# Binding the fetched-expert work behind its dense block on VectorE, and giving stored activations their own buffers

## The chip, the cores and the metric

One NeuronCore of a Trainium2 chip runs the whole program. The metric is the device time of one execution in microseconds. Before the change the median of three runs was 4709.95 us (4702.84 to 4711.42).

## What is computed

Two transformer-like blocks over 512 tokens of width 1024 in float32. The part that matters here is the expert layer ("PEER") of the first block. For each token and each of 8 heads, two top-16 searches over 128 keys give 16 of 16384 experts with softmax gates; the layer is a sum over these 128 experts per token:

```python
u_sel = u_tab[idx]
v_sel = v_tab[idx]
act = jax.nn.gelu(jnp.einsum('td,thkd->thk', hb, u_sel), approximate=False) * gate
return jnp.einsum('thk,thkd->td', act, v_sel)
```

The kernel computes it in two ways. For the last 384 tokens it is dense: all 16384 experts are evaluated in 128 blocks of 128, `gelu(u_tab @ x)` is multiplied by a matrix W that holds the gates (zero where an expert is not chosen), and the product goes through `v_tab`. For the first 128 tokens only the chosen rows of both tables are fetched: 128 rows of each table per token.

## The kernel before

Every float32 matrix product is made of three matmuls of rounded operands: `split` (L288) writes a high part with a cast on ScalarE (L294) and a low part with a subtraction on VectorE (L295), and `mm3` (L298) issues high x high, low x high and high x low (L300 to L302; names in the profile end in H and L). A weight tile is loaded in pairs (`wraw`, 1024 KB, two buffers) and split into `wd` or `we`.

`phase_b` calls three generators that are woven together by hand.

- `peer_select` (L1131) routes the tokens, and beside that computes the first NU = 56 of the 128 blocks of activations (`peer_act`, L1260: 24 matmuls of 384 columns, then a Gelu into a tile `pge`, three buffers) and stores them in HBM (`geD`). The matrix W goes to HBM too (`WD`).
- `peer_dense` (L1276) takes all 128 blocks in groups of four. A group is either *stored* (14 groups: its activations are loaded back from `geD` by `spilled`, L1286) or *fresh* (18 groups: `peer_act` computes them now, on PSUM bank `sb`); the two kinds alternate about evenly, and the last two groups are a stored and a fresh one. Each block's activations are multiplied by W in place (L1298, tile `pW`, one load per group), split into `pG` (three buffers), and drive 18 matmuls of 512 columns against the split rows of `v_tab` (`praw`, 1024 KB for two blocks, two buffers; `pV`, two buffers). The sums stay in six PSUM banks until the end.
- `peer_own` (L1085) is the work on fetched experts: 256 steps, each with one row of an expert table per token (128 x 1024 floats, 512 KB, an indirect DMA from GpSimd, L1111) in a ring of AHEAD = 4 buffers `pfr`. A step with a row of `u_tab` is a multiply-and-reduce on VectorE (L1119), a step with a row of `v_tab` a multiply-and-add into `pfo` (L1127); the order is 16 of the first kind, then alternately 16 and 16. After 16 dot products come a Gelu on ScalarE and a multiplication. The buffer freed by step k takes the row of step k + 4.

The steps of `peer_own` are handed out by counts. `peer_select` takes one per stored block from the fourth on, so `taken` is 53. `peer_dense` gets the other 203: a pace of 0.85 for a block that is followed by a stored one and 2.3 for one that is followed by a fresh one, scaled so that all are written by the 122nd block (L1312 to L1329).

What is written is not what is issued: the framework orders each engine's instructions by a priority that follows the program's order, among those that its own timing model holds ready. An instruction written later can so be issued earlier when the model sees its engine idle and its operands there. The order so found is fixed at build time; in the trace each engine's instructions run in one such order, and one that waits holds up those behind it. `issue_after(ins)` adds, for every instruction traced inside the block on the engine of `ins`, the condition that it be issued behind `ins`; it adds no instruction and no semaphore, and says nothing of instructions on other engines.

In the loop of `peer_dense`, the operands of block i + 1 (`nxt = next(G, None)`) are written before the matmuls of block i, and the own steps after them:

```python
(gh, gl), (vh, vl) = nxt, next(Vh)
nxt = next(G, None)
due += pace(i) * left / total
while gone < min(due, left):
    next(own)
    gone += 1
```

Of the kernel before, what the change touches and what calls it, by code (L numbers as in the profile page):

```python
# [9 lines left out]
F32 = mybir.dt.float32  # L10
# [20 lines left out]
TD = T - 128  # L31
# [221 lines left out]
class Kern:  # L253
# [34 lines left out]
    def split(self, pool, x, name, shape=None, bufs=1, l_eng=None):  # L288

        nc = self.nc  # L290
        shape = shape or list(x.shape)
        h = pool.tile(shape, F32R, name=name + 'H', bufs=bufs)
        l = pool.tile(shape, F32R, name=name + 'L', bufs=bufs)
        nc.scalar.copy(h, x)  # L294
        (l_eng or nc.vector).tensor_sub(l, x, h.bitcast(F32))  # L295
        return h, l

    def mm3(self, out, wh, wl, xh, xl, start, stop):  # L298
# [977 lines left out]
    def peer_dense(self, pd, f2, r, st, own):  # L1276


        nc, ap = self.nc, self.ap
        J = 4  # L1280

        ng, ns = 128 // J, NU // J
        order = sorted(range(ng), key=lambda i: (i + 0.5) / ns if i < ns else (i - ns + 0.5) / (ng - ns))
        fresh = self.peer_act(pd, f2, NU, 128 - NU, tag=('sb', 2))

        def spilled(grp):  # L1286
            for b in range(J * grp, J * grp + J):
                ge = pd.tile([128, TD], F32, name='pge', bufs=3)
                nc.sync.dma_start(ge, self.geD[b])
                yield b, ge  # L1290

        def acts():
            for grp in order:
                W = pd.tile([128, 12, J, 32], F32, name='pW', bufs=2)
                nc.sync.dma_start(W, self.WD[:, :, J * grp:J * grp + J, :])
                for b, ge in spilled(grp) if J * grp < NU else islice(fresh, J):
                    gv = ge.rearrange('p (a b) -> p a b', a=12)
                    nc.vector.tensor_mul(gv, gv, W[:, :, b % J])  # L1298
                    yield self.split(pd, ge, 'pG', bufs=3)

        def values():
            for grp in order:
                for i in range(0, J, 2):
                    raw = pd.tile([128, 2, 1024], F32, name='praw', bufs=2)
                    nc.sync.dma_start(raw, ap['pv'][128 * (J * grp + i):128 * (J * grp + i + 2)].rearrange('(t p) f -> p t f', t=2))
                    for q in range(2):
                        yield self.split(pd, raw[:, q], 'pV', bufs=2)

        acc = [[self.mmps() for _ in range(2)] for _ in range(2)] + [[self.mmps('sa', 2) for _ in range(2)]]
        G, Vh = acts(), values()  # L1310

        blocks = [grp * J >= NU for grp in order for _ in range(J)] + [False]  # L1312
        pace = lambda i: 2.3 if blocks[i + 1] else 0.85
        left = 256 - self.taken
        total = sum(pace(i) for i in range(122))
        due, gone = 0.0, 0
        nxt = next(G)
        for i in range(128):
            (gh, gl), (vh, vl) = nxt, next(Vh)
            nxt = next(G, None)  # L1320
            due += pace(i) * left / total

            for t, h in ([(t, h) for t in range(3) for h in range(2)] if i < 127 else [(t, h) for h in range(2) for t in range(3)]):
                s, c = slice(t * 128, t * 128 + 128), slice(h * 512, h * 512 + 512)
                self.mm3(acc[t][h], gh[:, s], gl[:, s], vh[:, c], vl[:, c], i == 0, i == 127)
            while gone < min(due, left):
                next(own)
                gone += 1
        for _ in own:  # L1329
            pass  # L1330

        o = [self.own] + [pd.tile([128, 1024], F32, name=f'po{t}') for t in range(3)]
        for h in range(2):
            c = slice(h * 512, h * 512 + 512)
            for t in range(3):
                (nc.scalar.copy, nc.vector.tensor_copy)[t % 2](o[t + 1][:, c], acc[t][h])
            for d in range(4 * h, 4 * h + 4):
                ps = self.mmps('sb', 2)
                for t in range(4):
                    nc.tensor.transpose(ps[:, t * 128:t * 128 + 128], o[t][:, d * 128:d * 128 + 128], self.ident)  # L1340
                nc.vector.scalar_tensor_tensor(r[:, d], ps, self.M[:, 40 + d, 0:1], r[:, d], op0=OP.mult, op1=OP.add)
                st.tile(d)
# [973 lines left out]
```

## Time and profile before

| | |
|---|---|
| median of three runs | 4709.95 us |
| the profiled execution, its own time | 4711.78 us |
| its span | 4709.2 us |
| busy: TensorE / VectorE / ScalarE / GpSimd | 93% / 58% / 35% / 22% |
| mean granted clock of TensorE | 0.959 of full speed |
| HBM traffic over the span | 137 GB/s |
| `peer_dense`: first and last multiplication by W (L1298) start at | 1482.5 and 2400.9 us |

The busy shares are means over stages with different limits. The stage of the change is about a fifth of the span, and it is read by itself, in two halves that look different: up to about 1960 us and from there on. A row of a wait says who waited, for whom, how long in total and how often. TensorE's matmuls are pipelined, so the sum of their durations is more than the time they take; what one costs in a full pipeline is read from the distance between starts.

### The profile page before, as it was taken

Reading aid. Unit: us, or ns where it says so; the run is one execution under the profiler, and the core shown is the slowest. Engines: PE = TensorE matmul, PEld = TensorE weight load, DVE = VectorE, ACT = ScalarE, POOL = GpSimd, SP = SyncE. Lnnn points to the kernel's source line nnn. Section 1 sums busy time; section 2 is a strip of 40 time slices with the busy share of each in tenths; the row PEclk is TensorE's granted clock in tenths of the full one; section 3 lists DMA queues with packets and bytes.
Section 4 is the critical chain, followed back from the end, with each engine's and each line's share of the span. In section 5 each row is a group of like instructions: output and inputs, shape, how many; then the busy total and the mean of one; then the engine's idle time right before and its main releaser. Section 6 shows DMA issues by size and latency. Waiting matters only on the chain. (4 is left out here: it accounts for less than half of the span.)

```text
span 4709.2 us, 58774 instructions
## 1 busy us (share of the span) xinstructions
PE 4389.7 (93%) x22821; PEld 3698.9 (79%) x22821; DVE 2741.0 (58%) x5167; ACT 1666.0 (35%) x2540; POOL 1048.5 (22%) x880
## 2 busy tenths in 40 slices
PE   7898998988887888999999999999999999999998
PEld 5776777878786776888878887788888888778887
DVE  5676577599987787644443357643343376636333
ACT  3533222326652222333332237332232242323222
POOL 3222343248784454200010021000110010001001
PEclk8899999999998999999999999999999999999999
DMA  6233423336679999745422222122322220011222
GB/s 220 81 97 110 146 106 128 117 113 227 231 272 350 328 327 334 253 170 177 172 70 99 94 90 90 59 90 98 100 81 98 92 76 15 16 45 63 99 95 75
DMA packets 226771, 647.50 MB, mean 137 GB/s; under 512 B 15587, under 2 KB 81395, under 8 KB 220092
## 3 DMA queue, kind: packets, MB, share of 16 engines
q1 hardware_dynamic: 188124, 502.18, 30.9%
q0 software_dynamic: 38368, 141.58, 8.3%
q8 instruction: 179, 2.93, 0.3%
q14 instruction: 100, 0.82, 0.1%
HBM read 590.66 MB, written 53.04 MB: 137 GB/s over the span
## 5 line engine op out<-in xcount | busy, mean ns | idle before, releaser
L302 PE MATMUL mm<-xH,wdL 128*128 128x512 f32 (+4 forms) x2276 | 850.3, 374 | 27.4 <-DVE wdL L295 27.2
L300 PE MATMUL mm<-xH,wdH 128*128 128x512 f32 (+4 forms) x2276 | 854.4, 378 | 15.0 <-DVE cacc L543 9.4
L301 PE MATMUL mm<-xL,wdH 128*128 128x512 f32 (+4 forms) x2276 | 850.4, 374 | 2.7 <-POOL xL L2292 1.5
L294 ACT CAST wdH<-wraw 128x1024 fp32r<-128x1024 f32 (+2 forms) x382 | 395.0, 1035 | 1156.1 <-PE mm L301 750.7
L295 DVE TENSOR_TENSOR wdL<-wraw,wdH 128x1024 fp32r<-128x1024 f32 (+2 forms) x346 | 421.7, 1219 | 460.5 <-ACT wdH L294 447.9
L302 PEld LDWEIGHTS mm<-xH,wdL 128*128 128x128 f32 (+2 forms) x2276 | 435.4, 191 | 99.1 <-DVE wdL L295 32.8
L300 PEld LDWEIGHTS mm<-xH,wdH 128*128 128x128 f32 (+2 forms) x2276 | 435.3, 192 | 86.6 <-issue 13.4
L301 PEld LDWEIGHTS mm<-xL,wdH 128*128 128x128 f32 (+2 forms) x2276 | 436.2, 192 | 70.0 <-POOL xL L2292 3.2
L294 ACT CAST weH<-wraw 128x1024 fp32r<-128x1024 f32 (+2 forms) x162 | 168.1, 1038 | 489.5 <-PE mm L301 302.7
L295 DVE TENSOR_TENSOR weL<-wraw,weH 128x1024 fp32r<-128x1024 f32 (+1 forms) x155 | 189.7, 1224 | 241.2 <-ACT weH L294 215.5
L300 PE MATMUL mm<-xH,weH 128*128 128x512 f32 (+2 forms) x856 | 319.5, 373 | 5.5 <-ACT weH L294 3.9
L302 PE MATMUL mm<-xH,weL 128*128 128x512 f32 (+2 forms) x856 | 316.6, 370 | 5.2 <-DVE weL L295 5.1
L301 PE MATMUL mm<-xL,weH 128*128 128x512 f32 (+2 forms) x856 | 317.5, 371 | 1.2 <-POOL xL L2292 1.1
L300 PE MATMUL mm<-pVH,pGH 128*128 128x512 f32 x512 | 210.8, 413 | 57.1 <-ACT pGH L294 48.4
L2210 POOL TENSOR_TENSOR nsa<-r 128x512 f32<-128x512 f32 x4 | 7.7, 1935 | 1042.9 <-DVE r L1373 1042.9
L2292 POOL TENSOR_TENSOR xL<-r,xH 128x256 fp32r<-128x256 f32 (+1 forms) x84 | 68.9, 832 | 760.1 <-DVE r L2279 499.7
L1366 DVE TENSOR_TENSOR fg<-fg,mm 128x512 f32<-128x512 f32 x88 | 60.5, 687 | 283.8 <-PE mm L302 283.1
L301 PE MATMUL mm<-pVL,pGH 128*128 128x512 f32 x512 | 210.7, 412 | 10.6 <-DVE pVL L295 10.6
L302 PE MATMUL mm<-pVH,pGL 128*128 128x512 f32 x512 | 212.2, 414 | 7.7 <-DVE pGL L295 7.5
L295 DVE TENSOR_TENSOR pVL<-praw,pVH 128x1024 fp32r<-128x1024 f32 x128 | 156.4, 1222 | 98.2 <-ACT pVH L294 98.2
L1111 POOL DMA_INDIRECT pfr<-in_pun_dram,pfI x128 | 167.6, 1310 | 154.9 <-DVE pfD L1119 90.4
L1111 POOL DMA_INDIRECT pfr<-in_pv_dram,pfI x128 | 164.9, 1289 | 158.6 <-DVE pfo L1127 103.2
(1244 smaller groups left out, 10041.7 us busy)
## 6 DMA issues: line engine op xcount, KB each, us to landing
wraw<-in_wi_dram SPq DMA_DIRECT2D x88, 1024.0 KB, 4.9
praw<-in_pv_dram SPq DMA_DIRECT2D x64, 1024.0 KB, 6.3
wraw<-in_pu_dram SPq DMA_DIRECT2D x63, 1024.0 KB, 6.0
wraw<-in_wmod_dram SPq DMA_DIRECT2D x24, 1024.0 KB, 6.7
wraw<-in_win_dram SPq DMA_DIRECT2D x24, 1024.0 KB, 5.7
WD<-W SPq DMA_DIRECT2D x12, 2048.0 KB
pW<-WD SPq DMA_DIRECT2D x32, 768.0 KB, 5.7
wraw<-in_wo_dram SPq DMA_DIRECT2D x16, 1024.0 KB, 5.0
```

What stands on the lines that cost most here:

```text
L294: nc.scalar.copy(h, x)
L295: (l_eng or nc.vector).tensor_sub(l, x, h.bitcast(F32))
L300: mm(out, wh, xh, start=start, stop=False)
L301: mm(out, wh, xl, start=False, stop=False)
L302: mm(out, wl, xh, start=False, stop=stop)
L1111: nc.gpsimd.indirect_dma_start(out=row, out_offset=None, in_=ap[n], in_offset=bass.IndirectOffsetOnAxis(ap=self.ownI[:, k:k + 1], axis=0))
L1366: nc.vector.tensor_mul(g, g, pss[0])
L2210: self.eng.tensor_add(self.sa, r[:, 0], r[:, 1])
L2292: eng.tensor_sub(l[:, k, s], F[k], h[:, k, s].bitcast(F32))
```

## The change

`split` keeps the VectorE subtraction that it issued last. In `peer_dense` the loop notes it after the operands of block i + 1 are written (so it is the subtraction that makes `pGL` of block i + 1), and the own steps written beside block i are bound behind it in VectorE's order. The stored activations get a tile name of their own, `pgs`, with four buffers; before, they shared the three buffers `pge` with the fresh ones, which now keep these for themselves.

```diff
-        (l_eng or nc.vector).tensor_sub(l, x, h.bitcast(F32))
+        self.last_split = (l_eng or nc.vector).tensor_sub(l, x, h.bitcast(F32)).ins
...
-                ge = pd.tile([128, TD], F32, name='pge', bufs=3)
+                ge = pd.tile([128, TD], F32, name='pgs', bufs=4)
                 nc.sync.dma_start(ge, self.geD[b])
...
             nxt = next(G, None)
+            mark = self.last_split
             due += pace(i) * left / total
...
             while gone < min(due, left):
-                next(own)
+                with self.tc.issue_after(mark):
+                    next(own)
                 gone += 1
```

## Rows read from the trace of the kernel before

**Rows 1.** the page's 40 slices: busy tenths of TensorE and of the DMA engines

```profile
PE   7898998988887888999999999999999999999998
...
DMA  6233423336679999745422222122322220011222
```

**Rows 2.** stretches: us, busy of PE, PEld, DVE, ACT, POOL; clock, DMA share, GB/s

```profile
1400.00:1480.00 80.00, 62.67 (x313) 59.69 (x311) 56.45 (x67) 17.57 (x27) 45.73 (x35) 0.91 0.95 345
1480.00:1960.00 480.00, 405.62 (x1778) 338.09 (x1779) 371.61 (x465) 132.97 (x186) 218.15 (x169) 0.92 0.90 329
1640.00:1680.00 40.00, 38.24 (x174) 32.72 (x174) 28.81 (x40) 10.40 (x14) 17.70 (x14) 0.95 0.86 312
1880.00:1920.00 40.00, 36.41 (x170) 31.65 (x170) 31.57 (x32) 11.34 (x15) 17.68 (x15) 0.96 0.85 314
1960.00:2400.00 440.00, 440.00 (x2151) 390.83 (x2150) 198.05 (x241) 159.43 (x214) 0.00 (x0) 1.00 0.49 164
```

**Rows 3.** the costliest group of TensorE's instructions, 1480 to 1960 us

```profile
L302 PE MATMUL mm<-pVH,pGL 128*128 128x512 f32 x236 | 104.0, 441 | 7.7 <-DVE pGL L295 7.5
```

**Rows 4.** timeline of TensorE around 2005 us: start, duration

```profile
2001.75 0.39 PE L300 MATMUL mm<-pVH,pGH 128*128 128x512 f32 x1
...
2005.87 0.33 PE L300 MATMUL sb<-xH,wdH 128*128 128x384 f32 x1
...
2010.06 0.39 PE L300 MATMUL mm<-pVH,pGH 128*128 128x512 f32 x1
```

**Rows 5.** row buffer pfr, 1400-1482, then 1482-2420 us: ns, first and last start

```profile
L1119 DVE CUSTOM_DVE_ANT_0 pfr<-pfr,pfh x19: 1215/1220/1226, 1399.5 to 1479.6; 128x1024 f32<-128x1024 f32 x19
L1127 DVE SCALAR_TENSOR_TENSOR pfo<-pfr,pfD,pfo x16: 1278/1284/1318, 1433.6 to 1467.6; 128x1024 f32<-128x1024 f32 x16
...
L1127 DVE SCALAR_TENSOR_TENSOR pfo<-pfr,pfD,pfo x96: 1271/1280/1325, 1525.3 to 1952.3; 128x1024 f32<-128x1024 f32 x96
L1119 DVE CUSTOM_DVE_ANT_0 pfr<-pfr,pfh x75: 1214/1220/1227, 1485.5 to 1857.3; 128x1024 f32<-128x1024 f32 x75
```

**Rows 6.** who waited for whom, 1480 to 1960 us: total us, times, longest

```profile
ACT pGH L294 <- DVE pge L1298: 258.0, 58, 9.5
...
PE mm L300 <- ACT pGH L294: 48.4, 17, 7.3
...
ACT pfD L1122 <- DVE pfD L1119: 11.5, 5, 6.8
```

**Rows 7.** DMA, 1480-1960: queues (packets, MB, share); issues (count, KB, us to landing)

```profile
q0 software_dynamic: 24507, 89.19, 50.5%
q1 hardware_dynamic: 41932, 68.35, 39.7%
...
praw<-in_pv_dram SPq DMA_DIRECT2D x30, 1024.0 KB, 9.6
wraw<-in_pu_dram SPq DMA_DIRECT2D x16, 1024.0 KB, 9.1
pW<-WD SPq DMA_DIRECT2D x15, 768.0 KB, 9.9
pge<-geD SPq DMA_DIRECT2D x28, 192.0 KB, 7.8
```

**Rows 8.** groups of VectorE's instructions, 1480-1960 us: busy, mean ns, idle

```profile
L1127 DVE SCALAR_TENSOR_TENSOR pfo<-pfr,pfD,pfo 128x1024 f32<-128x1024 f32 x96 | 123.0, 1281 | 38.3 <-DMA pfr<-in_pv_dram,pfI 37.8
L1119 DVE CUSTOM_DVE_ANT_0 pfr<-pfr,pfh 128x1024 f32<-128x1024 f32 x76 | 92.0, 1221 | 30.3 <-DMA pfr<-in_pun_dram,pfI 30.2
L295 DVE TENSOR_TENSOR pVL<-praw,pVH 128x1024 fp32r<-128x1024 f32 x61 | 74.3, 1219 | 6.8 <-ACT pVH L294 6.8
L1298 DVE TENSOR_TENSOR pge<-pge,pW 128x384 f32<-128x384 f32 x60 | 33.1, 553 | 30.4 <-DMA pge<-geD 28.8 <-DMA pW<-WD 1.6
L295 DVE TENSOR_TENSOR pGL<-pge,pGH 128x384 fp32r<-128x384 f32 x60 | 32.8, 551 | 1.2 <-ACT pGH L294 1.2
```

**Rows 9.** waits of SyncE's DMA queue, 1467 to 2420 us

```profile
SPq L1289 <- DVE pGL L295: 47.2, 23, 4.4
```

## The prediction

> **What bounds the kernel now.** I read the page's slices first. In slices 13 to 16 (1413 to 1884 us) TensorE is at seven or eight tenths and the DMA engines at nine; in slices 18 to 20 TensorE is at nine and the DMA engines at four or five [rows 1]. So the stage has a half that is short of transfers and one that is not. The stretches say how much: from 1480 to 1960 us TensorE is busy 405.62 of 480 us at a mean granted clock of 0.92 (between its two levels, 1.2 and 2.4 GHz) with the DMA engines at 0.90; from 1960 to 2400 us it is busy for all 440 us at 1.00, DMA at 0.49 [rows 2]. GpSimd, which does nothing here but fetch expert rows, has 169 instructions in the first half and none in the second.
>
> What the matmuls would take in a full pipeline comes from the timeline in the undisturbed half. 18 matmuls of 512 columns take 2005.87 - 2001.75 = 4.12 us (0.229 each), 24 of 384 columns 4.19 us (0.1746 each) [rows 4]. In the first half each of the three lines has 236 of the first kind on four of the six banks [rows 3], so 354 on all, 3 x 354 = 1062 in all, and 1778 - 1062 = 716 of the second [rows 2]: 243 + 125 = 368 us of work in 480 us. **112 us are lost there**, as idle time and as time at the lower clock that follows it. In the 80 us ahead of it (the last stored blocks of the selection, 313 matmuls of 384 columns) the work is 54.6 us, so 25 us are lost, at a DMA share of 0.95. Together 137 us; the second half loses nothing.
>
> The rows of the fetched experts say why. 171 own steps run after 1482 us, the last at 1952 us [rows 5]; 256 - 171 = 85 had run before, where only 53 are written. So 32 of the 35 steps between 1400 and 1482 us belong to dense blocks not yet begun, and all 256 are done when VectorE has split 61 of the 128 value blocks [rows 8], where the pace as written ends at the 122nd. In that half VectorE idles 37.8 us ahead of L1127 waiting for rows and 28.8 us ahead of L1298 for stored activations [rows 8]; ScalarE's cast behind L1298 waits 258.0 us, and 48.4 us of that reach TensorE [rows 6]. The steps come too early and too dense: they saturate the DMA engines, and VectorE, waiting in order for a late row, holds back the operands of the next block.
>
> **The change, part by part.** *The noted instruction* is bookkeeping at build time: 0 us.
>
> *The binding* adds no instruction and no wait; it forbids VectorE to issue a step written beside block i ahead of `pGL` of block i + 1. Some 203 steps then spread over 122 blocks. By the pace that is 0.85 for a stored block and 2.3 for a fresh one (54 x 0.85 + 68 x 2.3 = 202, so the scale is 1.00), over some 56 x 4.12 + 72 x 8.31 = 829 us of matmuls.
>
> First the 25 us ahead of the stage. Without the 32 rows (32 x 0.524 = 16.8 MB of the 27.6 that 345 GB/s move in 80 us) the DMA share falls from 0.95 to about 0.4, below the 0.49 at which TensorE never waits. I take all 25; the lower end is 10, if what is left waits on VectorE instead.
>
> Then the stage. Per block the transfers are [rows 7]: `praw` 0.524 MB, `pW` 0.197, for a stored block `pge` 0.197, for a fresh one `wraw` 0.524, and 0.524 per row. A stored block: 0.918 + 0.446 = 1.364 MB in 4.12 us, 331 GB/s; a fresh one: 1.245 + 1.21 = 2.455 MB in 8.31 us, 295 GB/s. Full share is 329 / 0.90 = 366 GB/s [rows 2], so the shares would be 0.90 and 0.81. What a row costs TensorE at a share is bounded by three rows. At 0.90 it is 112 / 171 = 0.65 us. In the two calmer stretches, share 0.86 and 0.85, I count 174 and 170 matmuls at the half's mean of 368 / 1778 = 0.207 us, 36.0 and 35.2 of 40 us, so 4.0 and 4.8 us for 14 and 15 rows: about 0.30 us each [rows 2]. At 0.49, without rows, nothing is lost. I price the 46 rows beside stored blocks at 0.65 (30 us), and the 157 beside fresh ones, below the calm stretches in share and at 0.28 rows per us against 0.36, at a quarter of 0.30 (11 us). **41 us stay of 137; the gain is 96.** The ends are 0 (gain 137) and 0.30 for all (61 us, gain 76); the 0.65 for all is a rival.
>
> What hides the rest: VectorE's load beside a stored block is 1.22 + 0.55 + 0.55 + 0.85 x 1.27 = 3.4 of 4.12 us, beside a fresh one 2.3 + 1.2 + 2.3 x 1.27 = 6.5 of 8.31 [rows 8]. It fits, but VectorE at 0.8 is late next, and a row that comes 1 us late beside a fresh block is still covered, two of 2 us are not. GpSimd's 256 fetches stay and are not bound; each waits for the buffer of the step four before, so with steps 3.6 to 4.8 us apart a row has some 14 us to land in. ScalarE's Gelu on 16 dots waits 11.5 us in 5 cases now, casts queued behind it [rows 6]; there are 6 or 7 such Gelus now instead of 5, the same price. The last steps are written two stored and four fresh blocks before the end, 41 us ahead of the transposes that read `pfo`.
>
> *The own buffers* cost 6 KB per partition and no instruction. The 56 loads leave SyncE's queue when the stored block four earlier is split, not when any of the last three blocks is; a group is loaded while the fresh group before it runs. That takes away the 28.8 us ahead of L1298 and most of the 47.2 us for which SyncE's queue stands still with `praw`, `pW` and `wraw` behind it [rows 9]; both are in the 112. Memory of the stage moves a little, so its first loads may wait for another tile of the selection: 0, with plus or minus 8 us as bounds (the longest wait of TensorE there is 7.3 [rows 6]).
>
> Sum: 4711.78 - 96 = 4616 for the profiled execution, which lies 1.8 us above the median: **4614 us.**
>
> A rule speaks for a higher price. The two queues held the engines 50.5% and 39.7% of the first half [rows 7]: the fetched rows, with a buffer always free, took more than half. The Trainium skill (DMA: Bandwidth & Descriptors, Queues, rings and completion order) says that each DMA engine takes turns, packet by packet, between the queues that have work for it. By that rule, with rows always queued, a stored block's 0.918 MB get half of 366 GB/s and take 5.0 us, 0.9 us too long; over 56 blocks 49 us would stay, a gain of 88. The trace agrees so far as both queues share nearly evenly; whether paced rows still keep the queue full no row shows.
>
> **The rivals.** *Stored groups stay short of transfers.* For it: 331 GB/s is what the saturated half moved. Against it: a stored group lasts only 16.5 us, and `praw`, `pW` and now `pgs` are a group ahead. Stored blocks at half of the engines' time (0.9 us each, 49 us) and fresh rows at the calm stretches' 0.30 (47 us) leave 96: gain 41, 4669 us.
>
> *The cost follows the row, not the crowding.* VectorE waits in order, and steps bound directly ahead of the next block's subtractions would now do so in the half where TensorE never waits. Each row then costs what it costs today, wherever it runs. It decides at 137 / 203 = 0.675 us per row: at 0.65 the gain is 5 (4705 us, no change); at the 25.4 / 35 = 0.73 of 1400 to 1482 us, 148 us are paid for 137: **slower, 4721 us.** Against it: the calm stretches pay half for as many rows.
>
> *The binding does not hold the steps back*, because rows already fetched move the crowding elsewhere. Then only the stored loads' part of VectorE's waits goes: 28.8 of 28.8 + 37.8 + 30.2 [rows 8], 30% of 112, 33 us: 4677 us. Against it: only four rows can be in flight.
>
> **How the numbers follow.** Forecast 0.71 (own range 4573 to 4640: gain 137 to 70); stored groups short 0.15; cost per row 0.09, half of it slower; no hold 0.05. Under 0.2% (9 us) a measurement of this kernel cannot tell a gain from none. Faster 0.91, same 0.05, slower 0.04. From 4578 to 4670 us lie nearly all of the forecast and about half of the first rival; above lie the rest.
>
> **What would show it.** Right: own steps on VectorE last to about 40 us before the stage's end; GpSimd busy through the stage; DMA share near 0.82 throughout; the stage's first and last L1298 some 850 us apart, not 918; the 80 us ahead of it shorter by 25; the wait for stored loads gone; landing of `praw` below 9.6 us. Wrong: the last own step still well ahead of the end, TensorE's idle spread over the whole stage behind L1127 and L1119, or a DMA share above 0.9 in stored groups.

## The result, and the profile after

The changed kernel takes 4583.03 us (median of 4 runs, 4576.06 to 4595.06) against 4710.0 us: a ratio of 0.9736 with the 95% interval [0.9709, 0.9763], 127 us faster. The prediction was 4614 us (4578 to 4670), so the result lies near the lower end of its range; on another chip, beside the first experiments, the same kernel gave 4578.69 us, 0.9729 [0.9705, 0.9754].

The page's slices after, to set beside [rows 1]:

```profile
span 4574.3 us, 58699 instructions
...
PE   7898899997889999999999999999999999999998
...
DMA  6233423336568888888423222222232210011222
```

The DMA engines no longer stand at nine tenths for four slices and at four or five soon behind them; they stand at eight for seven slices, and TensorE is at nine in each of these. The same in stretches (length, busy us of PE, PEld, DVE, ACT, POOL, granted clock, DMA share, GB/s), to set beside [rows 2]: the stage up to the last own step, the whole stage, and what follows the last own step.

```profile
1441.00:2223.00 782.00, 774.16 (x3750) 682.35 (x3749) 582.20 (x732) 280.99 (x385) 287.05 (x199) 1.00 0.87 308
1441.00:2265.00 824.00, 816.16 (x3956) 719.90 (x3955) 600.61 (x753) 295.63 (x403) 287.05 (x199) 1.00 0.84 297
2223.00:2265.00 42.00, 42.00 (x208) 37.56 (x207) 18.41 (x22) 14.64 (x20) 0.00 (x0) 1.00 0.29 101
```

TensorE is busy for 816 of 824 us at a granted clock of 1.00, the upper of its two levels, while the DMA engines carry 0.87 for 782 us. That is nearly the 0.90 of the old first half, which lost nearly a quarter of its 480 us (112 us).

The stored groups can be read by themselves, as the stretches of some 20 us in which bank `sb` gets next to no matmul, so that only the products with `v_tab` run (length, busy, clock, share and GB/s as above). Three of the fourteen:

```profile
1611.22:1631.50 20.28, 20.28 (x91) 16.74 (x90) 15.94 (x17) 7.70 (x11) 9.85 (x7) 1.00 0.96 336
...
1881.16:1901.44 20.28, 20.28 (x91) 16.73 (x90) 15.65 (x18) 7.69 (x11) 9.91 (x7) 1.00 1.01 365
...
2115.39:2135.68 20.29, 20.29 (x92) 16.74 (x91) 16.75 (x21) 7.71 (x11) 10.45 (x8) 1.00 0.99 369
```

In all of them but the last, which has next to no rows left, the DMA share is 0.93 to 1.04, and TensorE idles for under 2 us in each, in most not at all.

The own steps of the stage, with first and last start (compare [rows 5]):

```profile
L1127 DVE SCALAR_TENSOR_TENSOR pfo<-pfr,pfD,pfo x112: 1273/1279/1323, 1490.3 to 2223.8; 128x1024 f32<-128x1024 f32 x112
L1119 DVE CUSTOM_DVE_ANT_0 pfr<-pfr,pfh x91: 1211/1219/1227, 1446.4 to 2106.8; 128x1024 f32<-128x1024 f32 x91
```

All 203 lie in the stage now, and the last starts at 2223.8 us, 41 us before the last Gelu of the stage. VectorE hardly waits for their rows any more (1441 to 2223 us, compare [rows 8]):

```profile
L1127 DVE SCALAR_TENSOR_TENSOR pfo<-pfr,pfD,pfo 128x1024 f32<-128x1024 f32 x111 | 142.4, 1283 | 1.0
L1119 DVE CUSTOM_DVE_ANT_0 pfr<-pfr,pfh 128x1024 f32<-128x1024 f32 x91 | 108.2, 1219 | 5.8 <-DMA pfr<-in_pun_dram,pfI 5.8
...
L1298 DVE TENSOR_TENSOR pgs<-pgs,pW 128x384 f32<-128x384 f32 x56 | 29.5, 554 | 61.2 <-DMA pgs<-geD 48.5 <-DMA pW<-WD 12.5
```

38.3 and 30.3 us of idle time ahead of the own steps became 1.0 and 5.8. The wait for stored activations did not go: it grew from 28.8 to 48.5 us. But little of it reaches TensorE. Waits of the stage (total us, times, longest), the two longest and TensorE's own, to set beside [rows 6]:

```profile
POOL pfr L1111 <- DVE pfD L1119: 254.0, 49, 50.3
POOL pfr L1111 <- DVE pfo L1127: 251.7, 76, 14.6
...
PE mm L301 <- DVE pVL L295: 6.0, 6, 2.6
...
PE mm L300 <- ACT pGH L294: 1.8, 1, 1.8
```

TensorE waits 7.8 us in all where it waited 48.4 us for one cast alone; the longest waiter is now GpSimd, 505.7 us, for row buffers that VectorE has not yet used. Such waits alone are no sign that a pace holds: the run with no own step in the selection (below) has 502.0 us of them and loses 63 us. In the queues' shares, beside [rows 7], the fetched rows had 50.5% of the DMA engines against 39.7%, and have the smaller part now.

```profile
q1 hardware_dynamic: 82176, 135.61, 49.1%
q0 software_dynamic: 28656, 104.35, 37.2%
```

Where the time went is read from ScalarE's Gelus: those of the selection write from bank `mm`, those of the stage from `sb`. Before:

```profile
L1273 ACT ACTIVATE pge<-sb x72: 475/485/492, 1464.9 to 2399.6; 128x384 f32<-128x384 f32 x72
L1273 ACT ACTIVATE pge<-mm x56: 478/484/493, 1022.3 to 1463.5; 128x384 f32<-128x384 f32 x56
```

and after:

```profile
L1273 ACT ACTIVATE pge<-sb x72: 477/485/487, 1438.1 to 2264.9; 128x384 f32<-128x384 f32 x72
...
L1273 ACT ACTIVATE pge<-mm x56: 478/484/493, 1010.5 to 1433.9; 128x384 f32<-128x384 f32 x56
```

The selection went from 441.2 to 423.4 us, the stage from 934.7 to 826.8 us. These two make 126 us, the measured gain. The profiled execution also reaches the selection 11.8 us earlier, in a part that the change does not touch; other executions of kernels with the same earlier part reach it between 1010.5 and 1027.4 us, so that is a matter of the execution, and from here on I use the two lengths.

### The profile page after: what moved, and what is told of

Its sections match the earlier page's. It is cut to its first block, busy times and chain, and to the rows that moved or that the text cites. A ratio compares the mean times of both kernels' runs of the same rounds, so it can differ in the third digit from the quotient of the medians.

```text
span 4574.3 us, 58699 instructions
## 1 busy us (share of the span) xinstructions
PE 4337.6 (95%) x22821; PEld 3672.4 (80%) x22821; DVE 2737.0 (60%) x5167; ACT 1668.0 (36%) x2540; POOL 1079.5 (24%) x880
## 5 line engine op out<-in xcount | busy, mean ns | idle before, releaser
L1111 POOL DMA_INDIRECT pfr<-in_pun_dram,pfI x128 | 181.2, 1416 | 296.3 <-DVE pfD L1119 204.9
L1111 POOL DMA_INDIRECT pfr<-in_pv_dram,pfI x128 | 178.7, 1396 | 269.6 <-DVE pfo L1127 193.2
L302 PE MATMUL mm<-pVH,pGL 128*128 128x512 f32 x512 | 201.3, 393 | 0.0
L300 PE MATMUL mm<-pVH,pGH 128*128 128x512 f32 x512 | 196.4, 390 | 1.8 <-ACT pGH L294 1.8
L300 PEld LDWEIGHTS mm<-xH,weH 128*128 128x128 f32 x856 | 162.5, 190 | 31.6 <-ACT weH L294 4.6
```

The costliest lines, as they stand in the source:

```text
L300: mm(out, wh, xh, start=start, stop=False)
L302: mm(out, wl, xh, start=False, stop=stop)
L1111: nc.gpsimd.indirect_dma_start(out=row, out_offset=None, in_=ap[n], in_offset=bass.IndirectOffsetOnAxis(ap=self.ownI[:, k:k + 1], axis=0))
```

## The experiments

Each kernel was timed in three rounds beside the kernel before (4708 to 4710 us in the three sets) and profiled once. A summary, with the two lengths read as above:

| | median us | ratio to before, 95% | selection us | stage us |
|---|---|---|---|---|
| before | 4710.0 | | 441.2 | 934.7 |
| changed kernel, again | 4578.7 | 0.9729 [0.9705, 0.9754] | 420.3 | 826.0 |
| binding alone | 4628.8 | 0.9842 [0.9824, 0.9861] | 422.7 | 868.0 |
| own buffers alone | 4716.4 | 1.0015 [1.0000, 1.0030] | 443.6 | 941.9 |
| bound at the stage's start only | 4684.2 | 0.9956 [0.9941, 0.9971] | 422.4 | 929.1 |
| no own steps in the stage | 4570.4 | 0.9698 [0.9678, 0.9718] | 423.5 | 814.4 |
| bound, twice the pace | 4694.5 | 0.9968 [0.9953, 0.9983] | 423.9 | 937.5 |
| before, without the fetches | 4561.8 | 0.9676 [0.9653, 0.9698] | 407.7 | 817.8 |
| one ring of seven buffers | 4623.2 | 0.9812 [0.9796, 0.9828] | 422.0 | 869.0 |
| 26 steps in the selection | 4561.9 | 0.9680 [0.9660, 0.9699] | 394.6 | 834.4 |
| the same, flatter pace | 4574.5 | 0.9708 [0.9691, 0.9725] | 394.6 | 845.3 |
| 14 steps, flatter pace | 4592.2 | 0.9749 [0.9733, 0.9766] | 393.8 | 864.8 |
| none, flatter pace | 4608.4 | 0.9786 [0.9770, 0.9802] | 389.8 | 877.8 |

**The changed kernel again.**

> The changed kernel once more, on the chip of the next three. About 4583 us, 4576 to 4595 as before. Open beside it: in the profiles the selection begins 11.5 us earlier than before the change, in a part of the program that the change does not touch. If that is chance of one execution, this profile puts the first Gelu of the selection anywhere between 1010 and 1022 us; if the change moves the earlier order, it is near 1010 again.

4578.69 us, and the first Gelu of the selection starts at 1019.3 us: chance.

### Which of the two parts does it

**The binding alone.**

```diff
-                ge = pd.tile([128, TD], F32, name='pgs', bufs=4)
+                ge = pd.tile([128, TD], F32, name='pge', bufs=3)
```

> The binding alone, stored and fresh activations sharing three buffers as before. Theory (the steps came too early and too dense; the order is all): 4585 to 4600, at most 15 us above the changed kernel. Rival (the stored loads have a share of their own, priced at 28.8 of 96.8 us of VectorE's waits, 33 us): about 4615.

4628.8 us: a gain of 81, and 46 to 50 us short of both parts together. That is more than either theory gave the buffers. The waits of the stage in this kernel:

```profile
DVE pge L1298 <- DMA pge<-geD: 46.6, 16, 4.7
...
PE mm L300 <- ACT pGH L294: 20.0, 14, 2.8
PE mm L301 <- DVE pVL L295: 14.1, 11, 1.8
```

The wait for stored activations is no longer than in the changed kernel (46.6 against 48.5 us), and yet TensorE now waits 34.1 us where it waited 7.8. The place in VectorE's order accounts for that in the case that I followed. In this one of the 16 the loads leave SyncE's queue at 1568.20 us

```profile
1568.20 3.63 SPq L1289 DMA_DIRECT2D pge<-geD  x3
```

and the multiplication by W that needs the first of them stands directly in front of the split that the next matmuls need:

```profile
1577.54 0.56 DVE L1298 TENSOR_TENSOR pge<-pge,pW 128x384 f32<-128x384 f32 x1 [3.76 <-DMA pge<-geD]
1578.01 1.22 DVE L295 TENSOR_TENSOR pVL<-praw,pVH 128x1024 fp32r<-128x1024 f32 x1
```

In the changed kernel the stored tiles run far ahead:

```profile
L1298 DVE TENSOR_TENSOR pgs<-pgs,pW x56: 546/553/561, 1457.2 to 2186.3; 128x384 f32<-128x384 f32 x56
L294 ACT CAST pGH<-pgs x56: 506/516/518, 1461.2 to 2226.6; 128x384 fp32r<-128x384 f32 x56
```

The last of them is multiplied at 2186.3 us and cast at 2226.6 us, 40 us later; only the first four stand less than 25 us ahead of their casts. Waits in front of work that is this early cost TensorE next to nothing. The same idle row of VectorE is a cost in one kernel and none in the other, and its length does not tell which.

**The own buffers alone.**

```diff
-                with self.tc.issue_after(mark):
-                    next(own)
+                next(own)
```

> The four own buffers alone, no binding. Theory (order is all): 4700 to 4710, since VectorE still waits for rows that come late. Rival (a third of the loss is the stored loads): about 4677.

4716.4 us, no gain at all. From 1480 to 1960 us VectorE still waits 66.8 us for rows (68.0 before), its wait for stored activations is 31.2 us (28.8 before), and TensorE's for the cast behind L1298 is no shorter than in [rows 6]:

```profile
PE mm L300 <- ACT pGH L294: 55.1, 20, 7.3
```

The buffers are worth 46 to 50 us, but only once the binding has made room.

**More buffers, or a line of their own?**

```diff
-                ge = pd.tile([128, TD], F32, name='pgs', bufs=4)
+                ge = pd.tile([128, TD], F32, name='pge', bufs=7)
...
-            ge = tp.tile([128, TD], F32, name='pge', bufs=3)
+            ge = tp.tile([128, TD], F32, name='pge', bufs=3 if tag[0] == 'mm' else 7)
```

> The changed kernel with one shared ring of seven activation buffers instead of three and four. With one ring of three (the binding alone) the first load of a stored group leaves only when a fresh block has given a buffer back, 5.6 us before it is needed. Theory (the loads leave too late for want of free buffers): seven shared ones do as well as three and four, 4575 to 4595. Rival (what counts is that fresh and stored tiles do not wait in one line): 4610 to 4630 as with three.

4623.2 us: seven buffers in one ring do no better than three. My theory of too few buffers falls. The loads of a stored group now leave together, with no wait for a buffer in SyncE's queue, but still late:

```profile
1581.49 0.37 SPq L1305 DMA_DIRECT2D praw<-in_pv_dram  x1
1581.91 2.63 SPq L1289 DMA_DIRECT2D pge<-geD  x4
```

ScalarE's Gelu of the fresh block ahead of that group starts at 1582.24 us, 0.3 us from there, and VectorE's multiplication waits for the load until 1590.57 us. In one ring the tiles are handed out in the order in which they are written, so a load would not leave ahead of the fresh tile that is written before it. That reading fits the two times, but it is argued, not shown: in SyncE's queue the four loads also stand right behind a load of `praw` that had waited 5.7 us for its own buffer (first line), so the place in that queue would do as well. Shown is that seven buffers in one ring gain nothing over three, and three and four in two rings do; how many the ring of their own needs was not tried.

**Bound at the stage's start only.**

```diff
-            mark = self.last_split
+            mark = self.last_split if i == 0 else mark
```

> All own steps of the dense stage bound behind the first dense block only: none can run in the selection, but within the stage they are free to run early. Theory (crowding inside the stage costs 0.65 us per row, the selection's tail 25 to 29 us): the tail is gained back, but 203 rows instead of 171 crowd the first half, 32 x 0.65 = 21 us more, so 4695 to 4705. Rival (most of the gain is the tail and the start of the stage): about 4620.

4684.2 us, better than I expected. The selection has the changed kernel's length, so all of its 18 to 21 us come from keeping the 32 steps out of it. In the stage the crowding is back:

```profile
1445.00:1988.00 543.00, 468.44 (x2098) 392.94 (x2097) 429.32 (x542) 152.09 (x216) 271.75 (x199) 0.94 0.92 334
```

By the prediction's 0.207 us per matmul that is 434 us of work in 543, so 109 us for 203 rows, 0.54 each instead of the 0.65 that I put in.

### Transfers, VectorE's time, or the place of a step

**The steps without their fetches.** The kernel before, with three rows fetched once and read by every step:

```diff
-            row = rows[i]
+            row = rows[i % AHEAD]
...
-            fetch(i + AHEAD)
             yield
```

(AHEAD is 3 here, and the first kind of step writes its product to a tile of its own.)

> The kernel before, but only the first three rows are ever fetched and each own step reads one of them (so the sum for the first 128 tokens is another); all VectorE work of the steps stays, as early as the order makes it. Theory (transfers): VectorE alone has about 396 us of work in a half of 368, so some 28 us stay lost of 137: about 4600. Rival (VectorE's time for the early steps is the cost, not the transfers): 4690 to 4710.

4561.8 us. The steps are even earlier than before (the last starts at 1796.7 us instead of 1952.3), VectorE is busy for 79.7 of 80 us ahead of the stage, and TensorE hardly waits:

```profile
1400.00:1480.00 80.00, 79.69 (x418) 73.98 (x417) 79.72 (x103) 31.07 (x45) 0.00 (x0) 1.00 0.67 231
1480.00:1900.00 420.00, 418.69 (x2035) 369.55 (x2034) 359.25 (x449) 152.86 (x206) 0.00 (x0) 1.00 0.51 170
```

So neither early issue nor VectorE's time is the cost. Nearly the whole loss of the stage goes with the transfers (817.8 us against 814.4 with no own steps at all, below), and even the 28 us that I left to VectorE were not there. (The selection is without its fetches too, so the two kernels differ there by more than crowding.)

**Bound, but twice as dense.**

```diff
-        total = sum(pace(i) for i in range(122))
+        total = sum(pace(i) for i in range(61))
```

> The changed kernel with twice the pace: all 203 steps are written beside the first 61 blocks, still bound behind them and with the own buffers. Theory (transfers are what is short): 203 x 0.524 + 27 x 0.918 + 34 x 1.245 = 173 MB in 395 us of matmuls, at 366 GB/s 474 us, so 79 us lost: about 4660. Rival (the place of a step behind the block's operands is what saves, crowding is harmless): only VectorE's load counts, 440 us in 395, 45 us lost: about 4625, or 4585 if even that spreads.

4694.5 us. Every step is behind its block's operands and the stored activations have their buffers, and 112 to 116 us of the gain are gone:

```profile
1440.00:1900.00 460.00, 391.09 (x1713) 329.17 (x1712) 358.48 (x466) 128.00 (x178) 234.65 (x175) 0.92 0.92 335
```

The place of a step does not save the gain; what counts is how much the transfers ask for at a time. And the rate at which they saturate is not the 366 GB/s that I had from 329 / 0.90. The saturated stretches moved 329 GB/s before, 334 and 335 GB/s in these two kernels, with the DMA share at 0.90 to 0.92. By this kernel's own 335 GB/s the 173 MB of the expectation take 516 us for 395 us of matmuls: 121 us lost, and its stage lies 123 us above the 814.4 us of the next run.

**No own steps.**

```diff
-        left = 256 - self.taken
+        left = 0
...
-        for _ in own:
-            pass
```

> The changed kernel with the 203 own steps of the dense stage left out (no fetch, no work on VectorE; the first 128 tokens lack them). It is the floor of the stage. In the profile of the changed kernel the stage takes 824 us where its matmuls need 814.5, so if that count is right the floor is 4568 to 4575, about 10 us below the changed kernel, and a paced row costs 0.05 us. If the rows cost the 0.20 us each of the prediction, the floor is near 4540.

4570.4 us, and a stage of 814.4 us, 12 us shorter than the changed kernel's, in which a count of its matmuls at the prediction's two rates had shown 9.6 us lost of 824. By the medians 203 paced rows cost 8 to 13 us, 0.04 to 0.06 us each.

### How far the room goes

I took VectorE to bound part of the selection; then moving own steps from there into the stage should gain until the stage's transfers saturate.

**26 steps in the selection, 230 in the stage.**

```diff
-                if n > 9:
+                if n > 90:
```

> The changed kernel with 26 own steps instead of 53 taken in the selection, so 230 in the dense stage. From 1040 to 1390 us VectorE is busy for 38 to 39.9 of 40 us in most stretches, so 27 steps of 1.25 us less should shorten that by up to 33 us, and the stage pays 27 x 0.05 to 0.3 us: 4548 to 4570. Rival (the selection is held up by the order of the routing, not by VectorE's load, or the stage is then short of transfers): 4575 to 4595.

4561.9 us, 17 to 21 us below the changed kernel; the intervals of the two ratios, taken in different sets of runs, do not overlap, if only just (0.9699 and 0.9705). The selection is some 27 us shorter and the stage 8 longer.

```profile
L1273 ACT ACTIVATE pge<-sb x72: 477/485/487, 1414.6 to 2249.0; 128x384 f32<-128x384 f32 x72
...
L1273 ACT ACTIVATE pge<-mm x56: 480/483/504, 1015.8 to 1410.4; 128x384 f32<-128x384 f32 x56
```

That VectorE's time alone set the length of the selection is not borne out: in the kernel without fetches VectorE is busy for 384 of 408 us there, with 82 own steps, and in the changed kernel for 362 of 424 us with 53. The 27 rows moved also take 14 MB of transfers and GpSimd's work of fetching them out of the selection, and which of these gave the 27 us is open.

**The same with a flatter pace; 14 steps; none.** These also set

```diff
-        pace = lambda i: 2.3 if blocks[i + 1] else 0.85
+        pace = lambda i: 2.9 if blocks[i + 1] else 0.85
```

and `n > 126` and `n > 999`.

> 26 own steps in the selection as in the run that gave 4562, with the pace 0.85 and 2.9 instead of 2.3: fewer rows beside stored blocks (0.80 instead of 0.97 each), more beside fresh ones. Theory (stored blocks are where the share asked for is highest): 4552 to 4562. Rival (VectorE beside fresh blocks, 7 of 8.3 us, is then the bound): 4565 to 4580.

> 14 own steps in the selection, 242 in the dense stage, pace 0.85 and 2.9. Between the run with 26 and the one with none: theory 4550 to 4562, rival 4570 to 4590.

> No own step in the selection, all 256 in the dense stage, and the pace flatter in bytes per time (0.85 and 2.9 instead of 2.3, both scaled). 271 MB in 829 us of matmuls ask for a share of 0.89. Theory (paced transfers cost little as long as the share asked for is below one): the selection is 10 to 25 us shorter than with 26 taken (4562), the stage 5 to 15 longer: 4545 to 4565. Rival (near 0.9 the crowding returns, 0.3 us and more per row): 4590 or more.

4574.5, 4592.2 and 4608.4 us: all three are slower than 26 steps at the old pace (the first by little more than the noise: the intervals [0.9691, 0.9725] and [0.9660, 0.9699] touch, the stages differ by 11 us), and the theory that paced transfers stay cheap up to a share of one falls. The selection hardly shortens any more (394.6, 393.8, 389.8 us), and the stage pays 19.5 us for the next 12 rows and 32.5 us for the next 26, at least 1.25 us each. One row's transfer alone, 0.524 MB at 335 GB/s, is 1.56 us. Asked for per second of matmuls (829 us, as in the prediction) the stage's transfers come to 298 GB/s in the changed kernel, 315 with 230 rows, 323 with 242 and 332 with 256; the stage lies 12, 20 (31 with the flatter pace), 50 and 63 us above the floor. That the flatter pace costs 11 us at the same number of rows and the same mean is what my rival gave (4565 to 4580), by VectorE's load beside fresh blocks. What VectorE waits for rows in the stage grows with the loss, 19.0 us with 230 rows, 25.0 with the flatter pace, 41.6 with 242 and 56.9 with 256, where the changed kernel has 5.8; here the first and the last of these four:

```profile
DVE pfr L1119 <- DMA pfr<-in_pun_dram,pfI: 9.8, 8, 2.9
DVE pfo L1127 <- DMA pfr<-in_pv_dram,pfI: 9.2, 16, 1.6
...
DVE pfr L1119 <- DMA pfr<-in_pun_dram,pfI: 39.1, 31, 3.4
...
DVE pfo L1127 <- DMA pfr<-in_pv_dram,pfI: 17.8, 14, 2.7
```

That speaks for transfers, but VectorE's load grows as well, and these runs do not tell the two apart.

## Why the prediction was right, point by point

*Where the loss is, and how much.* Right. It put 137 us into the stage's first half and the tail of the selection. The floor of 814.4 us stands 120 us below the old stage, and the selection is 18 to 21 us shorter: 138 to 141 us.

*That early, dense steps saturate the transfers.* Right, and shown by the kernel without fetches (early and dense, hardly a loss) together with the one at twice the pace (bound, and the loss is back). The half-sentence on VectorE "waiting in order for a late row" is the way in which it reaches TensorE, not a cost of its own.

*The tail of the selection: all 25 us.* 18 to 21 us in the selection's length; the rest of the tail lies beyond its last Gelu, where the old stage begins, and is counted there (by the prediction's rate 17 us of the 25 are lost up to 1463.5 us and 8 behind).

*The pace and the end of the own steps.* Right: 203 steps, the last some 41 us before the end, GpSimd waiting for buffers.

*What a paced row costs: the term that was mis-sized.* I priced 46 rows beside stored blocks at 0.65 us, since these blocks ask for 331 GB/s, and 157 rows at 0.07: 41 us. The rows cost 8 to 13, and the first and last L1298 lie 824.8 us apart, not the forecast 850. The prediction took a share for a price and took it block by block. The stored groups did reach the share, 0.93 to 1.04 where 0.90 was forecast, and TensorE lost next to nothing in them: a group that asks for more than the mean seems to be carried by what was loaded ahead. The price rises with what the stage asks for: 0.04 to 0.06 us per row for 203 rows (298 GB/s), about 0.3 for each of the next 27 at the same pace (315 GB/s), and with the flatter pace at least 1.25 for each row beyond. That the mean over the stage decides is not shown, since at 230 rows the flatter pace, with the same mean, pays 11 us more. To be loaded ahead, the stored activations need the buffers of their own: without them the stage pays 42 us more (868.0 against 826.0), about the 41 that I had set for another reason. So the forecast of 4614 lies nearer to the binding alone (4628.8) than to the change.

*The buffers.* The prediction had them inside the 112 us and gave no price of their own in its sum; the 33 us of the last rival are not borne out, since alone they give nothing. Their worth depends on the binding: none without it, 46 to 50 us with it. And it said that the wait for stored loads would go; it grew, and moved to where it costs next to nothing. The same holds for SyncE's queue, whose standstill of 47.2 us [rows 9] was to go for the most part; it doubled:

```profile
SPq L1289 <- DVE pGL L295: 94.8, 37, 5.5
```

*The rule of taking turns.* With rows always queued a stored block would have lost 0.9 us, 49 us in all. The condition is not met: GpSimd spends 505.7 us waiting for buffers, and the rows' queue holds 37.2% of the engines, not half. That part of the Trainium skill (DMA: Bandwidth & Descriptors, Queues, rings and completion order), that a DMA engine takes turns between the queues with work for it, is neither borne out nor contradicted by the changed kernel. In the old first half 50.5% against 39.7% come near to it, but the prediction's words that a buffer was always free there misread the trace: GpSimd waited 216.8 of these 480 us for buffers,

```profile
POOL pfr L1111 <- DVE pfo L1127: 125.3, 67, 9.6
POOL pfr L1111 <- DVE pfD L1119: 91.5, 54, 6.5
```

and whether its queue was ever kept full is not shown.

*The rivals.* Stored groups short of transfers: no, TensorE is busy for 816 of 824 us, and nearly throughout in the stored groups. Cost by the row wherever it runs: no, 0.65 us before, 0.04 to 0.06 paced, none without transfers. No hold: no, the steps moved as written. One of the marks for being wrong came true all the same: the DMA share is above 0.9 in thirteen of the fourteen stored groups. It was a poor mark, by the same slip as the price of 0.65 us: a share is not a loss. How fast `praw` lands, a mark for being right, the trace after does not show.

## What to carry to other kernels

Work that is free to run early is not free if its transfers come along: bind it to the work that it is meant to hide beside, and look at the bytes that a stage asks for per time of its bounding engine, over what the buffers carry, before pricing a single block. Try a ring of their own for tiles that are loaded, apart from tiles that are computed: here seven buffers in one ring did no better than three; and read an idle row by how far ahead of its reader the waiting instruction stands, not by its length.

## What the runs showed of the hardware that was not expected

With several queues mixed, long stretches saturated at 329 to 335 GB/s with the DMA engines' share at 0.90 to 0.92 in three kernels, though shorter stretches reach more. In the changed kernel, at the start of the stage:

```profile
1440.00:1480.00 40.00, 39.80 (x190) 34.13 (x189) 32.78 (x51) 16.04 (x23) 15.52 (x11) 1.00 1.04 390
```

390 GB/s at a share of 1.04, and TensorE busy for 39.80 of 40 us; the thirteen stored groups, of some 20 us, move 336 to 386 GB/s. A short stretch at full share is no sign of a loss; dividing the rate of a long one by its share gave a ceiling, 366 GB/s, that no long stretch here reached.
